# Output projection of a hybrid trunk layer: products in sequence, operands formed earlier, gates eight tiles ahead

## The chip, the cores and the metric

The kernel runs on one core of a Trainium2 chip. The metric is the device time of one execution in microseconds (us). TensorE (PE) does the matrix products, VectorE (DVE) and ScalarE (ACT) the elementwise work, GpSimd (POOL) little besides issuing a few transfers, and SyncE (SP) issues most of them.

## The reference

One layer: two token mixers on a shared normalised input, merged by gates, projected, and followed by a per-layer embedding. All is float32, with 512 tokens and 2048 channels.

```python
h = rmsnorm(x, g_pre)
proj = h @ w_in                        # qkv, z_a, b, a, glu_in, z_b, gate_logits
...                                    # branch A: gated DeltaNet  -> o_a
y_a = o_a @ w_br_a
...                                    # branch B: GLU, depthwise conv, layernorm -> u
y_b = u @ w_br_b
gate_a, gate_b = split(sigmoid(gate_logits + b_gate), 2)
mixed = (gate_a * y_a + gate_b * y_b) @ w_out
x = x + rmsnorm(mixed, g_post)
e = p @ w_ple_proj
x = x + rmsnorm(sigmoid(x @ w_ple_gate) * e, g_ple)
```

The change concerns `gate_b`, `y_b`, the sum of the two gated branches, and the product with `w_out`.

## The kernel before, in words

**Products in float32.** Every operand of a matrix product is split into two halves, hi and lo: ScalarE copies it to the narrower type (hi), VectorE subtracts that from it (lo). A product is then hi·hi + hi·lo + lo·hi, three matmuls of 128 x 512 where one would stand.

**Tiles up to branch B.** `gemm_cm` queues one output tile: 128 channels by 512 tokens, 16 steps of 128 channels with three matmuls each, so 48 matmuls. Its weights come in two loads of 512 KB into the ring `raw`, which has three buffers, and are split into the ring `w`. The queue `jobs` is run in order. While it runs, side work is done by generators: `spawn(gen, period)` adds one, and each matmul of `gemm_cm` counts one tick, so that the generator takes one step every `period` matmuls. Instructions are written engine by engine in the order in which the program emits them; each engine and each queue works through its own in that order, and semaphores hold one that needs what is not there yet. The pools hold a new tile back until the last user of the memory below it is through.

**Branch B.** Two kinds of tiles alternate. `gate_b_tile(i)` multiplies the gate's weights with `hT`, and its evacuation (line 698) forms the sigmoid in a tile `gt` of the pool `slots`. The tile of `w_br_b` multiplies with `uT`, and its evacuation takes the gate times the bank (line 818) and adds it to `mixed[i]`, where the gated branch A lies (line 820). The gates run two tiles ahead of the tiles that use them. `mixed[i]` holds channels 128 i to 128 i + 127 of the sum, 512 tokens wide.

**w_out.** The matrix product with `w_out` is cut into 2 x 2 blocks, of the tokens (halves LO and HI of the columns of `mixed`) and of the channels (0 to 7 and 8 to 15), and seven products do the work of eight. Their names and token operands are P1 (A11), Q5 (S1), P6 (S2), P7 (S3), P3 (S4), P2 (A12) and Q4 (A22), where the S are sums and differences of blocks of `mixed`; their weights are B11 (P1), t = B11 + B12 (Q5), t + B22 (P6), B12 + B22 (P7), B22 (P3), B21 (P2) and t + B22 + B21 (Q4). The output columns are done in two halves, `jp` 0 and 1, and each product of a half has four pieces of weights of 128 x 1024; a piece gives 12 matmuls, so a product gives 48.

A piece passes through these steps. `stage` puts an entry for each of its four quarters q on a list; the entry (`e_a`, `e_b`, `e_c` and so on) issues the loads and sums when the list needs more sources. `load` (line 950) takes a buffer of `raw` for the first two kinds of pieces of half 0 and one of four buffers `rw` behind that; the `rw` and `t` tiles lie in the pool `s3`, which is opened over the space of the pool `s2` of branch B. The sum t is VectorE's (line 964), the blocks B22 and B21 are added to it by accumulating loads on GpSimd's queue (line 956), and P7's sum is VectorE's (line 973). `split_piece` splits a source on ScalarE (line 1010) and VectorE (line 1011) into two tiles `wsp`; three pieces, later four, are split ahead of the matmuls (lines 1034 to 1036, in `mms`).

`run(products, side)` takes the products piece by piece in turn. In half 0 the order before is P1 and Q5 in turn, then P6, P7 and P3 in turn, then P2 and Q4 in turn. The token operands A11 and S1 are formed by `split_a` (line 849 and on, through `sw_split`) when both of their rows of `mixed` are added, S3, S2 and S4 by `split_b` during P1 and Q5, and A12 and A22 by `split_c` during P6, P7 and P3. Behind w_out stand the post-norm, the transposes of its result and the product with `w_ple_gate`.

Of the kernel before, what the change touches and what calls it, by code (L numbers as in the profile page):

```python
# [81 lines left out]
def _body(ctx, tc, A, out):  # L82
# [756 lines left out]
    def split_a():  # L839
        for k2 in range(4):  # L840
            ah = hpool.tile([P, T], F32R, tag="h", name="ah")
            al = hpool.tile([P, T], F32R, tag="h", name="al")
            s1 = slots.tile([P, T], F32, tag="s", name="sf")
            for n in range(2):
                kk = 2 * k2 + n
                while not (kk in added and kk + 8 in added):
                    yield
                c = slice(n * 256, n * 256 + 256)
                nc.vector.tensor_tensor(s1[:, c], mixed[kk][:, HI], mixed[kk + 8][:, HI], ALU.subtract)
                nc.scalar.copy(ah[:, c], mixed[kk][:, LO])  # L850
                nc.vector.tensor_tensor(al[:, c], mixed[kk][:, LO], ah[:, c].bitcast(F32), ALU.subtract)
                yield
            Sf[k2] = s1
            AW["A11"][k2] = (ah, al)
            AW["S1"][k2] = sw_split(hpool, "h", s1)
            yield

    def split_b():
        for k2 in range(4):
            s1 = Sf.pop(k2)  # L860
            s3_ = s3.tile([P, T], F32, tag="s3", name="sf")
            for n in range(2):
                kk = 2 * k2 + n
                c = slice(n * 256, n * 256 + 256)
                nc.vector.tensor_tensor(s3_[:, c], mixed[kk][:, LO], mixed[kk][:, HI], ALU.subtract)
                nc.vector.tensor_tensor(s1[:, c], s1[:, c], mixed[kk][:, LO], ALU.subtract)
            AW["S3"][k2] = sw_split(hpool, "h", s3_)
            yield
            AW["S2"][k2] = sw_split(hpool, "h", s1)
            for n in range(2):  # L870
                kk = 2 * k2 + n
                c = slice(n * 256, n * 256 + 256)
                nc.vector.tensor_tensor(s1[:, c], mixed[kk + 8][:, LO], s1[:, c], ALU.add)
            AW["S4"][k2] = sw_split(slots, "s", s1)
            yield
# [8 lines left out]
    def gate_b_tile(i):  # L884
        gemm_cm(w_in_tile(GATE_TILE0 + 16 + i), hT, evac_gate(gate_b, i, 16 + i))

    gate_b_tile(order[0])
    gate_b_tile(order[1])
# [68 lines left out]

    def e_a(jp, q):
        early[0] = jp == 0
        b11 = load(jp, B11, q)  # L960
# [1 line left out]
        early[0] = False
        t = tb[q] = s3.tile([P, 1024], F32, tag="t", name="t", bufs=4)
        nc.vector.tensor_tensor(t, b11, b12, ALU.add)
        return [b11, t]
# [5 lines left out]
    def sum_t3(jp, q, b22):  # L971
        b12 = load(jp, B12, q)
        nc.vector.tensor_tensor(b12, b12, b22, ALU.add)
        return b12

    def e_b(jp, q):
        acc(tb[q], jp, B22, q)
        b22 = load(jp, B22, q)
        return [tb[q], sum_t3(jp, q, b22), b22]

    def e_p7(jp, q):
        return [sum_t3(jp, q, load(jp, B22, q))]
# [158 lines left out]
    gen = split_c()  # L1141
    ps = run(("P6", "P7", "P3"), stepper(gen))
    drain(gen)
    u2 = [add(unit(S3_, "u2"), ps["P6"][t], s1[t]) for t in range(2)]
# [192 lines left out]
```

## Time and profile before

| | before |
|---|---|
| median of 3 runs | 2548.74 us (2543.42 to 2550.84) |
| profiled execution, its own time | 2548.13 us |
| its span | 2546.4 us |
| granted clock of TensorE, mean | 0.998 |
| TensorE busy | 2503.4 us, 98% of the span |
| VectorE busy | 1650.9 us, 65% |
| ScalarE busy | 1058.2 us, 42% |
| 1840 to 2188, branch B: matmuls, GB/s | 1512, 94 |
| 2188 to 2393, w_out and the post-norm: matmuls, GB/s | 875, 225 |

The span is the stretch from the first to the last instruction that the profile holds; the execution's own time is 1.7 us longer. Times of day in this text are microseconds from the span's start. The matmuls overlap, so their durations (some 0.4 us each) add up to more than the time that passes: what one costs is the spacing of their starts. The granted clock is a share of the full 2.4 GHz; 0.50 is the lower level, 1.2 GHz. Below, w_out begins at 2188.98, right after the last evacuation of branch B.

### The profile page before, as it was taken

What the parts mean: (1) busy time and instruction counts of PE and PEld (TensorE: products, weight loads), DVE (VectorE), ACT (ScalarE), POOL (GpSimd) and SP (SyncE); (2) the same over time, 40 slices, a digit from 0 to 9 for tenths busy, and PEclk for the clock granted to TensorE, in tenths of its full rate; (3) what the DMA queues carried; (4) which work ended last, traced back from release to release, by engine and by line L of the source; (5) the groups of instructions that cost most, each with busy time, mean ns of one, the idle gap of its engine ahead of it and who ended that gap; (6) DMA issues with size and microseconds to landing.
All of it is one profiled execution on the core that took longest, in us unless ns stands there. A gap on an engine that the chain in (4) does not pass through costs nothing.

```text
span 2546.4 us, 32634 instructions
## 1 busy us (share of the span) xinstructions
PE 2503.4 (98%) x12202; PEld 2032.5 (80%) x12202; DVE 1650.9 (65%) x3092; ACT 1058.2 (42%) x2083; POOL 140.4 (6%) x151
## 2 busy tenths in 40 slices
PE   8999999999999999999999999999999999899998
PEld 7878787777878777888888888887888888687886
DVE  6766767666676765977786868947423333787744
ACT  6655455455545545322222222225422222454532
POOL 0100000000000000000000000002000000000000
PEclk9999999999999999999999999999999999999999
DMA  6322222222222222333333333342322223577642
GB/s 256 118 90 71 84 74 80 79 78 84 71 83 72 83 69 81 103 101 106 98 104 100 103 108 96 108 161 91 100 98 93 99 91 99 165 218 213 216 173 75
DMA packets 85406, 279.45 MB, mean 110 GB/s; under 512 B 9472, under 2 KB 9728, under 8 KB 85248
## 3 DMA queue, kind: packets, MB, share of 16 engines
q1 hardware_dynamic: 81792, 266.89, 31.3%
q0 software_dynamic: 2304, 8.39, 1.9%
q10 hardware_dynamic: 1152, 2.10, 0.3%
q8 instruction: 95, 1.56, 0.3%
q14 instruction: 63, 0.52, 0.1%
HBM read 262.66 MB, written 14.68 MB: 109 GB/s over the span
## 4 chain that ended last, share of the span: by engine, by line
PE 84%; DVE 9%; ACT 2%; issue 2%; DMA 2%; POOL 0%; SPq 0%; DVEq 0%; POOLq 0%; ACTq 0%
PE g L180 22%; PE g L178 22%; PE g L176 22%; DVE prod L589 2%; DVE w L124 2%; PE f L1191 2%; PE f L1192 2%; PE f L1190 2%; DVE VT L590 2%; PE psS L467 1%; PE f L1035 1%; PE f L1036 1%; PE f L1034 1%; DVE cv L404 1%; PE psB L462 1%
## 5 line engine op out<-in xcount | busy, mean ns | idle before, releaser
L180 PE MATMUL g<-hh,w 128*128 128x512 f32 x2320 | 919.4, 396 | 13.2 <-DVE w L124 13.2
L178 PE MATMUL g<-hl,w 128*128 128x512 f32 x2320 | 915.9, 395 | 0.0
L176 PE MATMUL g<-hh,w 128*128 128x512 f32 x2320 | 914.5, 394 | 0.0
L124 DVE TENSOR_TENSOR w<-raw,w 128x512 fp32r<-128x512 f32 x780 | 547.8, 705 | 491.8 <-ACT w L123 490.7
L123 ACT CAST w<-raw 128x512 fp32r<-128x512 f32 x780 | 479.1, 620 | 899.2 <-PE g L180 822.6
L180 PEld LDWEIGHTS g<-hh,w 128*128 128x128 f32 x2320 | 436.7, 188 | 107.0 <-DVE w L124 21.4
L178 PEld LDWEIGHTS g<-hl,w 128*128 128x128 f32 x2320 | 436.6, 188 | 87.3 <-issue 1.6
L176 PEld LDWEIGHTS g<-hh,w 128*128 128x128 f32 x2320 | 436.6, 188 | 83.7 <-issue 0.2
L671 DVE SCALAR_TENSOR_TENSOR uc<-sg,vec,uc 128x483 f32<-128x483 f32 (+15 forms) x480 | 351.3, 734 | 14.2 <-ACT uc L668 4.3
L404 DVE SCALAR_TENSOR_TENSOR cv<-g,vec,cv 128x511 f32<-128x511 f32 x144 | 107.0, 743 | 32.9 <-ACT cv L402 32.3
L180 PE MATMUL g<-uh,w 128*128 128x512 f32 x256 | 100.9, 394 | 0.0
L176 PE MATMUL g<-oh,w 128*128 128x512 f32 x256 | 100.9, 394 | 0.0
L178 PE MATMUL g<-ol,w 128*128 128x512 f32 x256 | 100.9, 394 | 0.0
L180 PE MATMUL g<-oh,w 128*128 128x512 f32 x256 | 100.9, 394 | 0.0
L176 PE MATMUL g<-uh,w 128*128 128x512 f32 x256 | 100.9, 394 | 0.0
L178 PE MATMUL g<-ul,w 128*128 128x512 f32 x256 | 100.9, 394 | 0.0
L589 DVE TENSOR_TENSOR prod<-UT,VT 128x2 f32<-128x2 f32 (+30 forms) x248 | 87.8, 354 | 7.2
L1034 PE MATMUL f<-wsp,oph 128*128 128x512 f32 x192 | 74.9, 394 | 3.2 <-ACT wsp L1010 3.2
L1035 PE MATMUL f<-wsp,oph 128*128 128x512 f32 x192 | 75.7, 394 | 1.5 <-DVE wsp L1011 1.5
L1191 PE MATMUL f<-w,xh 128*128 128x512 f32 x192 | 75.1, 391 | 0.1
L1036 PE MATMUL f<-wsp,opl 128*128 128x512 f32 x192 | 75.1, 391 | 0.0
L1192 PE MATMUL f<-w,xl 128*128 128x512 f32 x192 | 75.0, 390 | 0.0
(297 smaller groups left out, 2678.2 us busy)
## 6 DMA issues: line engine op xcount, KB each, us to landing
raw<-in_w_in SPq DMA_DIRECT2D x290, 512.0 KB, 3.3
raw<-in_w_ple_gate SPq DMA_DIRECT2D x40, 512.0 KB, 4.0
rw<-in_w_out SPq DMA_DIRECT2D x36, 512.0 KB, 5.0
raw<-in_w_br_a SPq DMA_DIRECT2D x32, 512.0 KB, 3.3
raw<-in_w_br_b SPq DMA_DIRECT2D x32, 512.0 KB, 3.2
t<-in_w_out POOLq DMA_DIRECT2D x16, 512.0 KB, 7.3
x<-in_x SPq DMA_DIRECT2D x8, 512.0 KB, 9.4
pe_dram<-e_sb SPq DMA_DIRECT2D x16, 256.0 KB, 5.6
```

Source lines behind the costliest of these rows:

```text
L123: nc.scalar.copy(hi, rq)
L124: nc.vector.tensor_tensor(lo, rq, hi.bitcast(F32), ALU.subtract)
L176: mm(ps, wh, rh, start=(k == 0), stop=False)
L178: mm(ps, wh, rl, start=False, stop=False)
L180: mm(ps, wl, rh, start=False, stop=(k == NK - 1))
L404: nc.vector.scalar_tensor_tensor(y[:, s:], ps[:, 0:T - s], vv(w0 + 3 - s), y[:, s:], ALU.mult, ALU.add)
L589: nc.vector.tensor_tensor(pv_, um, vm, ALU.mult)
L671: nc.vector.scalar_tensor_tensor(y[:, s:], u[:, 0:T - s], vv(w0 + TAPS - 1 - s), y[:, s:], ALU.mult, ALU.add)
L1035: mm(ps, lh, wl[:, c], start=False, stop=False)
L1036: mm(ps, ll, wh[:, c], start=False, stop=kk == 7)
L1191: mm(ps[tt], lh, wl, start=False, stop=False)
L1192: mm(ps[tt], ll, wh, start=False, stop=k == NK - 1)
```

## The change

- The gates run eight tiles ahead (`AHEAD = 8`) and, but for the first two, lie in the pool `s2`.
- `split_a`, `split_b` and `split_c` become `combine(k2)`, which forms all token operands of two rows of `mixed` and their partners but the split of S3. The generator over `combine(0)` to `combine(2)` starts behind the ninth of the 16 tiles of `w_br_b` (all gates are through by then), with a step every 12 matmuls; `combine(3)` runs during P1, three steps a piece; the splits of S3 run during P2.
- The order of half 0 is now P1, P2, Q5, P6, P7, P3, Q4, one product after the other. P1's piece is B11 and P2's is B21, both without a sum.
- The sum t is no longer formed from two loaded pieces on the way to Q5, but during P2: B12 is loaded into the t tile itself (line 979), and the kept piece of P1 is added to it (line 980). P7 loads B22 and B12 for itself (line 1000 is its sum), P3 loads B22 again.
- The first nine pieces' splits, before eight, lie in the ring `w` and in `wx`; the second load of x goes to `slots`, before to `hpool`.

The diff, cut to its core:

```diff
-    def evac_gate(dst, i, col):
+    def evac_gate(dst, i, col, pool=None):
         def f(ps):
-            gt = slots.tile([P, T], F32, tag="s", name="gt")
+            gt = (pool or slots).tile([P, T], F32, tag="s2" if pool else "s", name="gt")
...
+    def combine(k2):
+        ah = hpool.tile([P, T], F32R, tag="h", name="ah")
+        al = hpool.tile([P, T], F32R, tag="h", name="al")
+        for kk, c in halves(k2):
+            while not (kk in added and kk + 8 in added):
+                yield
+            nc.scalar.copy(ah[:, c], mixed[kk][:, LO])
+            nc.vector.tensor_tensor(al[:, c], mixed[kk][:, LO], ah[:, c].bitcast(F32), ALU.subtract)
+            yield
+        AW["A11"][k2] = (ah, al)
+        for kk, c in halves(k2):
+            CC[kk] = sw_split(hpool, "h", mixed[kk + 8])
+            yield
+        s1 = slots.tile([P, T], F32, tag="s", name="sf")
+        for kk, c in halves(k2):
+            nc.vector.tensor_tensor(s1[:, c], mixed[kk][:, HI], mixed[kk + 8][:, HI], ALU.subtract)
+        AW["S1"][k2] = sw_split(hpool, "h", s1)
+        yield
+        s3_ = slots.tile([P, T], F32, tag="s", name="sf")
+        s4 = slots.tile([P, T], F32, tag="s", name="sf")
+        for kk, c in halves(k2):
+            nc.vector.tensor_tensor(s3_[:, c], mixed[kk][:, LO], mixed[kk][:, HI], ALU.subtract)
+            nc.vector.tensor_tensor(s1[:, c], s1[:, c], mixed[kk][:, LO], ALU.subtract)
+        yield
+        for kk, c in halves(k2):
+            nc.vector.tensor_tensor(s4[:, c], mixed[kk + 8][:, LO], s1[:, c], ALU.add)
+        AW["S2"][k2] = sw_split(slots, "s", s1)
+        yield
+        AW["S4"][k2] = sw_split(slots, "s", s4)
+        Sf[k2] = s3_
+        yield
...
     jobs.append(finish)
+    for n in range(2, AHEAD):
+        gate_b_tile(order[n], s2)
     for n, i in enumerate(order):
-        if n + 2 < NK:
-            gate_b_tile(order[n + 2])
-        elif n == NK - 2:
-            jobs.append(lambda: spawn(split_a(), 6, "mix"))
         gemm_cm(A["w_br_b"][i], uT, evac_yb(i))
+        if n + AHEAD < NK:
+            gate_b_tile(order[n + AHEAD], s2)
+        elif n + AHEAD == NK:
+            jobs.append(lambda: spawn(split_mixed(), 12, "mix"))
...
+    def e_p1(jp, q):
+        early[0] = True
+        first[q] = load(jp, B11, q)
+        early[0] = False
+        return [first[q]]
+
+    def e_p2_t1(jp, q):
+        b21 = load(jp, B21, q)
+        t = t_tile(q)
+        nc.sync.dma_start(t, WO[jp, B12, q])
+        nc.vector.tensor_tensor(t, t, first.pop(q), ALU.add)
+        return [b21]
...
-            if n < 8:
+            if n < 9:
...
-                xr[tt, j] = unit(HP_, "xr")
+                xr[tt, j] = unit(SLOT, "xr")
...
-    for e, jp in ((e_a, 0), (e_b, 0), (e_c, 0), (e_a, 1), (e_63, 1), (e_p2, 1), (e_p7, 1), (e_t, 1)):
+    for e, jp in ((e_p1, 0), (e_p2_t1, 0), (e_t, 0), (e_p6, 0), (e_p7, 0), (e_p3, 0), (e_q4, 0), (e_a, 1), (e_63, 1), (e_p2, 1), (e_p7, 1), (e_t, 1)):
         stage(e, jp)
...
-    gen = split_b()
-    ps = run(("P1", "Q5"), stepper(gen))
+    gen = combine(3)
+    ps = run(("P1",), stepper(gen, 3))
     drain(gen)
     s1 = [snap(S3_, x) for x in ps["P1"]]
-    s5 = [snap(S3_, x) for x in ps["Q5"]]
+    gen = split_s3()
+    ps = run(("P2",), stepper(gen))
+    drain(gen)
+    c11 = [add(unit(S3_, "c11"), ps["P2"][t], s1[t]) for t in range(2)]
...
+    ps = run(("Q5",))
+    s5 = [snap(S3_, x) for x in ps["Q5"]]
+    ps = run(("P6",))
...
```

**Place 1.** SP's loads at the end of branch B and the start of w_out. `raw` are pieces of the ring with three buffers, `rw` and `t` pieces in `s3`; the numbers count tiles. Before:

```order
L950 DMA raw_17421<-in_w_out 128x1024
L950 DMA raw_17423<-in_w_out 128x1024
L950 DMA raw_17431<-in_w_out 128x1024
L950 DMA rw_17585<-in_w_out 128x1024
L950 DMA rw_17587<-in_w_out 128x1024
L950 DMA raw_17433<-in_w_out 128x1024
L950 DMA raw_17468<-in_w_out 128x1024
L950 DMA rw_17680<-in_w_out 128x1024
```

and in the changed kernel:

```order
L956 DMA raw_17480<-in_w_out 128x1024
L956 DMA raw_17482<-in_w_out 128x1024
L956 DMA raw_17488<-in_w_out 128x1024
L956 DMA rw_17524<-in_w_out 128x1024
L979 DMA t_17526<-in_w_out 128x1024
L956 DMA rw_17562<-in_w_out 128x1024
L979 DMA t_17564<-in_w_out 128x1024
L956 DMA rw_17593<-in_w_out 128x1024
L956 DMA raw_17494<-in_w_out 128x1024
L979 DMA t_17595<-in_w_out 128x1024
L956 DMA rw_17618<-in_w_out 128x1024
```

Three raw loads stand ahead in both. Before, raw loads of the next pieces follow behind two loads of P7 and P3; now the fourth raw load, P1's last piece, stands behind three rw loads of P2 and two loads of B12 into t tiles.

**Place 2.** VectorE from the last evacuation of branch B on. Line 818 is the gate times the bank, line 820 the last addition to `mixed`, 1011 (before) and 1034 (after) the low half of a piece of weights. Before:

```order
L1011 TENSOR_TENSOR wsp_17428<-raw_17421,wsp_17427 128x1024
L818 TENSOR_TENSOR gt_17159<-g_17330,gt_17159 128x512
L964 TENSOR_TENSOR t_17425<-raw_17421,raw_17423 128x1024
L820 TENSOR_TENSOR gt_13133<-gt_13133,gt_17159 128x512
L1011 TENSOR_TENSOR wsp_17442<-raw_17431,wsp_17441 128x1024
L849 TENSOR_TENSOR sf_17357<-gt_10733,gt_13133 128x256
L1011 TENSOR_TENSOR wsp_17438<-t_17425,wsp_17437 128x1024
```

and in the changed kernel, where nine rows are left out (the split of P1's third piece and eight instructions of `combine(3)`):

```order
L818 TENSOR_TENSOR gt_16824<-g_17406,gt_16824 128x512
L1034 TENSOR_TENSOR wsp_17491<-raw_17482,wsp_17490 128x1024
L820 TENSOR_TENSOR gt_13133<-gt_13133,gt_16824 128x512
...
L980 TENSOR_TENSOR t_17526<-t_17526,raw_17480 128x1024
L836 TENSOR_TENSOR opl_17591<-sf_17557,oph_17589 128x512
L1034 TENSOR_TENSOR wsp_17599<-rw_17562,wsp_17598 128x1024
L980 TENSOR_TENSOR t_17564<-t_17564,raw_17482 128x1024
L1034 TENSOR_TENSOR wsp_17530<-raw_17494,wsp_17529 128x1024
L1034 TENSOR_TENSOR wsp_17568<-rw_17524,wsp_17567 128x1024
```

The sum t stood right behind the last evacuation; now the first sum stands behind the operand work, and the split of P1's fourth piece (`raw_17494`) behind the second sum. The sum reads `raw_17480`, whose buffer that fourth piece takes.

**Place 3.** VectorE ahead of Q5's last piece in the changed kernel, `t_17620`. Line 1083 adds P1 to P2, line 1103 multiplies with g_post, line 1000 is a sum of P7's weights:

```order
L1083 TENSOR_TENSOR c11_17705<-f_17627,snap_17614 128x512
L1034 TENSOR_TENSOR wsp_17720<-t_17595,wsp_17719 128x1024
L1083 TENSOR_TENSOR c11_17707<-f_17628,snap_17616 128x512
L1000 TENSOR_TENSOR rw_17843<-rw_17843,rw_17841 128x1024
L1103 TENSOR_TENSOR c11_17705<-c11_17705,grow_17709 128x512
L1103 TENSOR_TENSOR c11_17707<-c11_17707,grow_17709 128x512
L1034 TENSOR_TENSOR wsp_17725<-t_17620,wsp_17724 128x1024
```

and before, around one of P7's sums (there line 973):

```order
L1011 TENSOR_TENSOR wsp_17712<-rw_17682,wsp_17711 128x1024
L836 TENSOR_TENSOR opl_17665<-sf_17357,oph_17663 128x512
L973 TENSOR_TENSOR rw_17736<-rw_17736,rw_17734 128x1024
L836 TENSOR_TENSOR opl_17709<-gt_11033,oph_17707 128x512
L1011 TENSOR_TENSOR wsp_17740<-rw_17680,wsp_17739 128x1024
```

A sum of P7 now stands ahead of a split that Q5, two products earlier, needs.

## Rows read from the trace of the kernel before

**Rows 1.** Page, busy us of each engine, share of the span, instructions.

```profile
PE 2503.4 (98%) x12202; PEld 2032.5 (80%) x12202; DVE 1650.9 (65%) x3092; ACT 1058.2 (42%) x2083; POOL 140.4 (6%) x151
```

**Rows 2.** Windows: stretch, its us, busy us of engines, granted clock, DMA share, GB/s.

```profile
2100.00:2150.00 50.00, 50.00 (x219) 40.78 (x218) 16.58 (x27) 13.02 (x23) 0.00 (x0) 1.00 0.29 95
2150.00:2200.00 50.00, 47.98 (x204) 37.66 (x203) 30.53 (x55) 17.70 (x29) 1.06 (x1) 1.00 0.41 131
2200.00:2250.00 50.00, 45.55 (x193) 35.74 (x193) 45.42 (x60) 29.32 (x39) 6.07 (x7) 1.00 0.82 214
2250.00:2300.00 50.00, 50.00 (x220) 41.05 (x220) 36.85 (x41) 26.03 (x39) 5.20 (x6) 1.00 0.76 220
```

**Rows 3.** All waits of TensorE, 1840 to 2320: us in total, times, longest.

```profile
PE f L1034 <- ACT wsp L1010: 3.9, 4, 2.0
PE f L1035 <- DVE wsp L1011: 1.5, 2, 1.0
PE f L1034 <- DVE gt L818: 0.9, 1, 0.9
```

**Rows 4.** TensorE's timeline: start, us, instruction, [idle before <-releaser].

```profile
2188.98 0.47 PE L1034 MATMUL f<-wsp,ah 128*128 128x512 f32 x1 [0.88 <-DVE gt L818]
...
2204.63 0.74 PE L1034 MATMUL f<-wsp,oph 128*128 128x512 f32 x2 [2.03 <-ACT wsp L1010]
...
2340.55 0.44 PE L1113 MATMUL x1t<-cst,snap 128*128 128x128 f32 x2 [2.38 <-DVE snap L1107]
```

**Rows 5.** ScalarE's group, 2188 to 2320: count | busy, mean ns | idle before.

```profile
L1010 ACT CAST wsp<-t 128x1024 fp32r<-128x1024 f32 x20 | 21.0, 1050 | 26.9 <-PE f L1035 10.8 <-DVE t L964 8.8 <-PE f L1036 7.2
```

**Rows 6.** VectorE's timeline at the seam of branch B and w_out.

```profile
2188.75 1.22 DVE L964 TENSOR_TENSOR t<-raw 128x1024 f32<-128x1024 f32 x1
2189.88 0.68 DVE L820 TENSOR_TENSOR gt<-gt 128x512 f32<-128x512 f32 x1
2190.48 1.22 DVE L1011 TENSOR_TENSOR wsp<-raw,wsp 128x1024 fp32r<-128x1024 f32 x1
2191.61 0.42 DVE L849 TENSOR_TENSOR sf<-gt 128x256 f32<-128x256 f32 x1
```

**Rows 7.** SP's timeline at the seam.

```profile
2167.11 11.58 SPq L950 DMA_DIRECT2D raw<-in_w_out  x3
2188.18 0.81 SPq L950 DMA_DIRECT2D rw<-in_w_out  x2
2190.03 0.80 SPq L950 DMA_DIRECT2D raw<-in_w_out  x2
```

**Rows 8.** DMA issues at 2188.1, 2190.0 and 2190.8: KB each, us to landing.

```profile
rw<-in_w_out SPq DMA_DIRECT2D x1, 512.0 KB, 3.5
...
raw<-in_w_out SPq DMA_DIRECT2D x1, 512.0 KB, 5.5
...
rw<-in_w_out SPq DMA_DIRECT2D x1, 512.0 KB, 7.3
```

**Rows 9.** A window behind a longer wait, in an earlier stage.

```profile
954.00:957.00 3.00, 3.00 (x9) 2.32 (x8) 2.08 (x5) 2.90 (x5) 0.00 (x0) 0.50 0.51 175
```

**Rows 10.** TensorE's timeline there, first and last of ten matmuls.

```profile
953.47 0.61 PE L180 MATMUL g<-hh,w 128*128 128x512 f32 x1 [2.83 <-DVE w L124]
...
957.22 0.40 PE L180 MATMUL g<-hh,w 128*128 128x512 f32 x1
```

**Rows 11.** DMA issues 2219.5 to 2221 and 2207 to 2207.5.

```profile
grow<-in_g_post ACTq DMA_DIRECT2D x2, 256.0 KB, 7.5
rw<-in_w_out SPq DMA_DIRECT2D x1, 512.0 KB, 6.9
...
t<-in_w_out POOLq DMA_DIRECT2D x1, 512.0 KB, 5.4
```

**Rows 12.** DMA issues 2280 to 2292.

```profile
t<-in_w_out POOLq DMA_DIRECT2D x4, 512.0 KB, 8.8
rw<-in_w_out SPq DMA_DIRECT2D x3, 512.0 KB, 16.2
```

More of the change, by code (lines that the diff above doesn't have):

```diff
@@ L837, in sw_split @@
         return hi, lo
-    def split_a():
-        for k2 in range(4):
[L841 to L875, printed above, removed]
@@ L877, in split_c, with halves @@
-    def split_c():
-        for kk in range(8):
-            CC[kk] = sw_split(*((slots, "s") if kk < 4 else (s3, "s3")), mixed[kk + 8])
+    def halves(k2):
+        for n in range(2):
+            yield 2 * k2 + n, slice(n * 256, n * 256 + 256)
+    def combine(k2):
[29 more added lines that the diff above has]
+        yield
@@ L880, in split_c, with split_mixed, split_s3, gate_b_tile @@
+    def split_mixed():
+        for k2 in range(3):
+            yield from combine(k2)
+    def split_s3():
+        for k2 in range(4):
+            AW["S3"][k2] = sw_split(s3, "s3", Sf.pop(k2))
             yield
     order = [k + 8 * n for k in range(8) for n in range(2)]
[L884 to L888, printed above, removed]
+    AHEAD = 8
+    def gate_b_tile(i, pool):
+        gemm_cm(w_in_tile(GATE_TILE0 + 16 + i), hT, evac_gate(gate_b, i, 16 + i, pool))
@@ L956, in acc, with t_tile, e_p6 @@
         nc.gpsimd.dma_start(t, WO[jp, blk, q], accum_op=ALU.add)
+    first = {}
+    def t_tile(q):
+        tb[q] = s3.tile([P, 1024], F32, tag="t", name="t", bufs=4)
+        return tb[q]
+    def e_p1(jp, q):
[9 more added lines that the diff above has]
+        return [b21]
     def e_a(jp, q):
-        early[0] = jp == 0
         b11 = load(jp, B11, q)
         b12 = load(jp, B12, q)
[L962 to L965, printed above, removed]
+        nc.vector.tensor_tensor(t_tile(q), b11, b12, ALU.add)
+        return [b11, tb[q]]
+    def e_p6(jp, q):
+        acc(tb[q], jp, B22, q)
+        return [tb[q]]
     def e_63(jp, q):
@@ L969, in e_63, with e_p7, e_p3 @@
         return [tb[q], load(jp, B22, q)]
-    def sum_t3(jp, q, b22):
+    def e_p7(jp, q):
+        b22 = load(jp, B22, q)
         b12 = load(jp, B12, q)
         nc.vector.tensor_tensor(b12, b12, b22, ALU.add)
[L974 to L982, printed above, removed]
+        return [b12]
+    def e_p3(jp, q):
+        return [load(jp, B22, q)]
     def e_p2(jp, q):
@@ L986, in e_p2, with e_q4 @@
         return [load(jp, B21, q)]
+    def e_q4(jp, q):
+        acc(tb[q], jp, B21, q)
+        return [tb[q]]
     def e_t(jp, q):
         return [tb[q]]
-    def e_c(jp, q):
-        return e_p2(jp, q) + [tb[q]]
     def split_piece():
@@ L1129, in drain @@
             pass
-    for e, jp in ((e_a, 0), (e_b, 0), (e_c, 0), (e_a, 1), (e_63, 1), (e_p2, 1), (e_p7, 1), (e_t, 1)):
+    for e, jp in ((e_p1, 0), (e_p2_t1, 0), (e_t, 0), (e_p6, 0), (e_p7, 0), (e_p3, 0), (e_q4, 0), (e_a, 1), (e_63, 1), (e_p2, 1), (e_p7, 1), (e_t, 1)):
         stage(e, jp)
-    gen = split_b()
-    ps = run(("P1", "Q5"), stepper(gen))
+    gen = combine(3)
+    ps = run(("P1",), stepper(gen, 3))
     drain(gen)
     s1 = [snap(S3_, x) for x in ps["P1"]]
-    s5 = [snap(S3_, x) for x in ps["Q5"]]
+    gen = split_s3()
+    ps = run(("P2",), stepper(gen))
+    drain(gen)
+    c11 = [add(unit(S3_, "c11"), ps["P2"][t], s1[t]) for t in range(2)]
     gp = [bcast_row(A["g_post"], j) for j in (0, 1)]
     fin = out_fin(0, gp)
[L1141 to L1144, printed above, removed]
+    for t in range(2):
+        fin(t, 0, c11[t])
+    ps = run(("Q5",))
+    s5 = [snap(S3_, x) for x in ps["Q5"]]
+    ps = run(("P6",))
+    u2 = [add(s1[t], ps["P6"][t], s1[t]) for t in range(2)]
     d = [minus(unit(S3_, "d"), s5[t], u2[t]) for t in range(2)]
+    ps = run(("P7",))
     u3 = [add(u2[t], ps["P7"][t], u2[t]) for t in range(2)]
     for t in range(2):
+        fin(2 + t, 1, minus(s5[t], s5[t], u3[t]))
+    ps = run(("P3",))
+    for t in range(2):
         fin(t, 1, add(d[t], ps["P3"][t], d[t]))
-        fin(2 + t, 1, minus(s5[t], s5[t], u3[t]))
-    ps = run(("P2", "Q4"))
-    for t in range(2):
-        fin(t, 0, add(s1[t], ps["P2"][t], s1[t]))
+    ps = run(("Q4",))
     for t in range(2):
```

2 lines of the change are left out of this document (added).

## The prediction

> **What bounds the kernel now.** I read the busy shares first: TensorE is busy 98% of the span [rows 1], so only its waits can be won. The table by windows then shows where they lie around the change: no loss through branch B, the loss in 2150 to 2250, none in 2250 to 2300 [rows 2]. The waits of TensorE name who ended them [rows 3], and its timeline gives the places [rows 4]: 0.9 us at the start of w_out, then short waits for split pieces of weights in the first two products (P1, Q5, piece by piece in turn), the longest 2.03, six of them after the first. Together these are 6.3 us [rows 3]. By counts it is more: the two windows hold 204 and 193 matmuls where undisturbed ones hold 219 and 220, 42 too few, at 50/220 = 0.227 us 9.5 us [rows 2]. A few records can be missing, and a matmul after a wait is followed by longer spacing, so I take 9.0: 1.0 at the start and 8.0 behind. That is the most this change can win there, 0.3% of the time. A later 2.4 us, before the transposes of x1 [rows 4], waits on the post-norm chain, which stays.
>
> **The change part by part.**
>
> *Gates eight tiles ahead.* The same 32 tiles of 48 matmuls run in another order. All waits of TensorE from 1840 to 2320 are the three lines of [rows 3], none of them in branch B, and VectorE and ScalarE are busy 16.6 and 13.0 of 50 us there [rows 2]. Cost 0.
>
> *Operands formed in branch B.* Three of four combinations move ahead of w_out. One is, on VectorE, five instructions of 512 columns at 0.68 and ten of 256 at 0.42 [rows 6], 7.6 us, and less on ScalarE. Three are 23 us of VectorE in the seven tiles that follow (seven times 48 matmuls at 0.227, 76 us), where two thirds of it is free: cost 0; if that cover were gone a piece would be late by one such instruction, 0.7. What it takes out of 2187 to 2225 is what made pieces late there: VectorE was busy 45.4 of 50 [rows 2]. So those six waits go: minus 8.0.
>
> *What is late next: the fourth piece of P1.* P1 alone now needs 36 matmuls for its first three pieces, 36 x 0.227 = 8.2 us from 2188.98 [rows 4], so the fourth is due at 2197.2. Its load goes into a raw buffer, of which there are three; the first three hold the pieces 0 to 2, and buffer 0 is now read once more, by the sum t = B12 + B11 (line 980), which waits for a new load of B12. Before, B12's load had come in the same raw ring long before, and the sum stood right behind the last evacuation [rows 6]. Now (order of SP and VectorE, places 1 and 2):
> - The loads into rw and t now lie over space that held a gate: they wait for the last addition of branch B, line 820. In VectorE's order a 1024-wide split stands ahead of it, as the sum did before, so it ends at 2189.88 + 0.68 = 2190.6 [rows 6]. Before, the first rw load went at 2188.18 [rows 7].
> - First load at 2190.6, t's at 2191.0 (issues stand 0.4 apart [rows 7]). A load issued alone took 3.5, and the third and the fifth in line landed at 2190.0 + 5.5 and 2190.9 + 7.3, 1.35 for each place [rows 8]. So t lands at 2195.5.
> - VectorE ahead of the sum: the split of piece 2 after ScalarE's 1.05 (to 2192.8), then operand work of 0.6, 0.6, 4 x 0.34 and 0.6 (starts in a row stand that much closer than the durations [rows 6]), to 2196.0; the sum takes 1.22 and ends at 2197.2 [rows 6].
> - The raw load goes at 2197.2, sixth in the queue: 2190.6 + 3.5 + 5 x 1.35 = 2200.8, and alone it would need 3.5, 2200.7.
> - ScalarE splits a piece of t ahead of it, which waits for the second sum (t, fourth in the queue, lands at 2198.2; a split on VectorE and the sum end at 2200.4): 2201.4, then its own 1.05: 2202.5 [rows 5]. VectorE's low half comes 1.22 later, 2203.7 [rows 6].
> - TensorE waits from 2197.2 to 2202.5, 5.3, runs two matmuls, and waits again to 2203.7, 0.7: together 6.0. Bounds: 4 if the splits ahead cost nothing (2200.8 to the first matmul, and half of the rest), 8 if the loads share the engines with other traffic and land 2 us later.
>
> Here a page can be set beside the row. Loads queued on SP landed 1.35 us apart [rows 8]. The Trainium skill's DMA: Bandwidth & Descriptors, Anatomy of one DMA, fits a transfer by 2.0 us and its bytes over 436 GB/s, measured on the GpSimd path; taken as an estimate for SP's loads that is 1.2 us each and 2.0 once. By it the sixth load would land at 2199.8, but not before the sum lets it go, 2197.2 + 3.2 = 2200.4: the wait would be about 0.4 us shorter. No run here shows 436 GB/s on such a load.
>
> *The clock.* The short waits left the granted clock at 1.00 [rows 2]. The one wait of 2.83 us, at 953, did not: the clock stood at 0.50, which is the lower level, for 954 to 957 [rows 9], and the matmuls from 953.47 to 957.22, nine spacings, took 3.75 us instead of 2.04, so 1.7 us [rows 10]. A wait of 5.5 us should do the same. I take 1.7, with 0 and 2 as bounds (part of it can fall inside the wait).
>
> *The queue of sums behind.* Four more loads of 512 KB (B12 comes twice), 4 x 1.35 us of queue. P7's sums (line 1000) each wait for two loads, and the third stands ahead of Q5's last split on VectorE (place 3). One of its loads needs a buffer that the second sum frees, and that sum one that the split of P2's last piece frees: eight VectorE instructions of 1.13 and one of 0.6 (their spacing in [rows 6]) behind 2202.5 in the order, 2212.2; its load 3.5 to 4 later, its sum at 2217.2, 28.2 us into w_out. With an accumulating load and two g_post rows in flight a load took 6.9 [rows 11], so it lands at 35.1; its sum 1.2, g_post's two products 1.2 and the split 1.2 make 38.7. TensorE, after 132 matmuls, needs it at 6.0 + 1.7 + 132 x 0.227 = 37.7. So 1.0; bounds 0 (landing in under 6) and 4. P7's third piece is held the same way by the fourth sum, with some 2 us to spare after it; 0.5, bounds 0 and 4.
>
> *Kept or nothing.* The start still waits for the last evacuation: the first bank is its bank, 1.0 as before. Matmuls and splits are as many as before. x's second load goes to other buffers and into other places of SP's order; the product before the transposes may wait, bounds minus 1 and plus 2, taken 0.
>
> **Sum**, against the profiled execution's 2548.13 (the span 2546.4 plus 1.7 around it): minus 8.0, plus 6.0, 1.7, 1.0 and 0.5, is plus 1.2: 2549.3. The median of the runs shown, 2548.74, lies 0.6 above that execution, so 2549.9; I say 2550.
>
> **Rivals.** A measurement of this kernel tells about 0.3%, 7.6 us, from no change: faster is below 2541.1, slower above 2556.4.
>
> *It does what it says.* The pieces of both products are there in time and w_out runs from its start: 2548.7 - 8.0 = 2540.7. For it: three raws land well before the start as now (three loads over 2167 to 2178 [rows 7]), and the operands are ready. It needs the fourth raw load to go at 2188 and not behind the sum. Against it: the order, where SP has that load behind rw and t loads that cannot go before branch B ends, and the re-read of buffer 0.
>
> *Loads collide.* The sums of P7 stand in VectorE's order ahead of splits of earlier products. If their loads meet the accumulating loads, several of which are now issued within a few us, TensorE waits for a load. Three loads issued over 2280 to 2292 had a median of 16.2 us to landing beside four accumulating ones at 8.8 [rows 12]. With 16.2 in place of 6.9 the wait at Q5's last piece is 1.0 + 9.3: 2559. It decides from some 13 us to landing on. Against it: before, such loads at up to 16 us fell into 2250 to 2300, at 220 GB/s, and TensorE lost nothing there [rows 2]. The Trainium skill, Trainium Kernel Development and Optimization, Key Constraints, has DMAs of all queues run on the same 16 engines and interleave, which is this rival's ground; the 5.4 us of an accumulating load alone against 8.8 among others agrees [rows 11, 12].
>
> **How the numbers follow.** Forecast 0.77, from 2545 to 2556 by its bounds, all of it within 0.3%. It does what it says 0.07: faster 0.05, the rest within. Loads collide 0.16: slower. So faster 0.05, same 0.79, slower 0.16. The range takes in most of both rivals' near sides: 2544.5 to 2558.
>
> **What would show it.** The waits of TensorE in the first 35 us of w_out: right, if the six short ones are gone and one of 4.5 to 7 us stands at P1's fourth piece, ended by ScalarE's split, with that load issued some 9 us into w_out right after the first sum; and if the granted clock falls to 0.50 behind it. Q5's last split should end a wait of 0 to 4. Wrong, if the fourth raw load goes with the first rw loads, if P1 has no wait over 2 us, or if a wait over 3 us stands in branch B or beyond P7.

## The result, and the profile after

The changed kernel takes 2554.28 us (median of 11 runs, 2549.91 to 2558.34), the kernel before 2547.28 in the same runs. The ratio is 1.0027, with a 95% interval of 1.0018 to 1.0036: 5 to 9 us slower. The forecast was 2550, the range 2544.5 to 2558. The profiled execution took 2554.67, its span is 2552.9 us and its mean granted clock 0.996.

The waits of TensorE in half 0 (the columns are those of [rows 3]) show the six short ones gone and two long ones in their place, the first where the forecast had it:

```profile
PE f L1057 <- ACT wsp L1033: 5.3, 1, 5.3
PE f L1058 <- DVE wsp L1034: 4.1, 2, 3.6
PE f L1057 <- DVE gt L818: 0.9, 1, 0.9
```

Its timeline has the places, as [rows 4] had them before: the start of w_out, P1's last piece, Q5's last piece, and at the end of w_out two waits close together.

```profile
2186.50 0.47 PE L1057 MATMUL f<-wsp,ah 128*128 128x512 f32 x1 [0.88 <-DVE gt L818]
2200.34 1.22 PE L1057 MATMUL f<-wsp,ah 128*128 128x512 f32 x2 [5.32 <-ACT wsp L1033]
2228.22 0.80 PE L1058 MATMUL f<-wsp,oph 128*128 128x512 f32 x1 [3.59 <-DVE wsp L1034]
...
2342.22 0.50 PE L1058 MATMUL f<-wsp,oph 128*128 128x512 f32 x1 [1.35 <-DVE wsp L1034]
...
2344.80 0.69 PE L1136 MATMUL x1t<-cst,c 128*128 128x128 f32 x2 [1.38 <-DVE c L1130]
```

Windows behind these waits have the clock at its lower level, called the half clock below (the third number from the end, 0.50). Before, it stayed at 1.00 all through w_out, up to 2300 by [rows 2] and from 2300 to 2400 by two more such windows.

```profile
2201.00:2203.50 2.50, 2.46 (x7) 1.51 (x6) 2.50 (x3) 0.23 (x1) 0.00 (x0) 0.50 0.87 354
2228.50:2231.00 2.50, 2.50 (x7) 1.92 (x8) 2.50 (x3) 0.24 (x1) 1.96 (x3) 0.50 0.46 56
2346.00:2350.00 4.00, 4.00 (x14) 3.28 (x13) 3.56 (x6) 1.39 (x3) 0.00 (x0) 0.50 0.53 183
```

What each product loses is counted from the starts in TensorE's timeline: 48 matmuls at an undisturbed spacing of 0.2286 us take 10.97 us, and what 48 starts take beyond that is the loss, waits and half clock together. Loss in us, in the order of each kernel; "end" are the last two of w_out's 14 products, among which the transposes stand, so that their own time is in it. The start's 1.0 is in none.

| kernel | half 0 by product | half 0 | end |
|---|---|---|---|
| before | P1 and Q5 in turn 7.3, then 0.7 | 8.0 | 6.1 |
| changed | P1 7.5, P2 0, Q5 5.2, P6 0, P7 1.1, P3 0, Q4 0 | 13.7 | 9.5 |
| changed, second profile (e8) | P1 8.5, Q5 5.6, P7 0.3 | 14.3 | 8.2 |
| e1 | P1 0.1, P2 1.3, P7 4.7 | 6.1 | 5.7 |
| e2 | P1 7.8, P7 0.3 | 8.1 | 5.2 |
| e3 | P1 and Q5 in turn 9.0 | 9.0 | 4.7 |
| e4 | P1 7.5, Q5 4.7, P7 1.7 | 13.8 | 7.3 |
| e5 | P1 0.1, P2 1.0, P7 3.8 | 4.8 | 6.0 |
| e6 | P1 0.1, P7 5.3 | 5.3 | 5.5 |
| e7 | P1 8.2, Q5 2.0, P7 4.8 | 15.0 | 7.3 |
| e9 | P1 0.1, P7 and P3 in turn 1.9 | 2.0 | 9.3 |
| e10 | P1 8.6, P7 and P3 in turn 1.2 | 9.8 | 6.5 |
| e11 | P1 and Q5 in turn 9.2, then 1.4 | 10.5 | 4.9 |
| e12 | P1 0.1, P7 and P3 in turn 1.9 | 2.0 | 5.1 |

So of the two profiled executions the changed one loses 5.7 us more in half 0 and 3.4 more at the end, 9.1; from the start of w_out to the end of the span it is 366.4 against 357.4. The spans differ by 6.5 only, since w_out began at 2186.50 instead of 2188.98. That is no gain of the change: branch B takes the same time in both, the 2.4 us stand before it, where the same work runs, and over all the profiles here w_out began between 2186.5 and 2189.5. Some 1.6 of the 2.4 are the half clock behind the wait of 2.83 us at 953 [rows 9, 10]. The changed kernel's execution has the same wait there, and behind it the clock stayed at 1.00:

```profile
952.65 0.50 PE L180 MATMUL g<-hh,w 128*128 128x512 f32 x1 [2.76 <-DVE w L124]
...
952.50:956.00 3.50, 3.35 (x15) 2.77 (x16) 2.55 (x6) 2.72 (x4) 0.00 (x0) 1.00 0.41 150
```

In the 14 profiles this wait is 2.74 to 2.85 us long; the half clock stands behind it in eleven and not in three (changed, e4, e10). So a half clock behind a wait of this size can differ between executions of the same work, and part of a difference between two rows of the table is that.

### The profile page after: what moved, and what is told of

The parts are those of the page before. It is cut to its first block, busy times and chain, and to the rows that moved or that the text cites. A ratio compares the mean times of both kernels' runs of the same rounds, so it can differ in the third digit from the quotient of the medians.

```text
span 2552.9 us, 32648 instructions
## 1 busy us (share of the span) xinstructions
PE 2506.6 (98%) x12202; PEld 2036.1 (80%) x12202; DVE 1652.8 (65%) x3092; ACT 1062.4 (42%) x2083; POOL 140.6 (6%) x151
## 4 chain that ended last, share of the span: by engine, by line
PE 84%; DVE 9%; issue 3%; ACT 2%; DMA 2%; POOL 0%; SPq 0%; DVEq 0%; POOLq 0%; ACTq 0%
PE g L180 22%; PE g L178 22%; PE g L176 22%; DVE prod L589 2%; DVE w L124 2%; PE f L1221 2%; PE f L1220 2%; PE f L1219 2%; DVE VT L590 2%; PE psS L467 1%; PE f L1058 1%; PE f L1057 1%; DMA rw<-in_w_out 1%; PE f L1059 1%; DVE cv L404 1%
## 5 line engine op out<-in xcount | busy, mean ns | idle before, releaser
L671 DVE SCALAR_TENSOR_TENSOR uc<-sg,vec,uc 128x483 f32<-128x483 f32 (+15 forms) x480 | 351.7, 735 | 14.3 <-ACT uc L668 4.3
```

Of the source, the lines that this page charges most:

```text
L671: nc.vector.scalar_tensor_tensor(y[:, s:], u[:, 0:T - s], vv(w0 + TAPS - 1 - s), y[:, s:], ALU.mult, ALU.add)
```

## The experiments

The ratios are to the kernel before, timed on the same chip.

**e1, P1's fourth piece.**

```diff
     def e_p1(jp, q):
-        early[0] = True
+        early[0] = q < 3
```

> The changed kernel, with P1's fourth piece loaded into an rw buffer in place of a raw one, so that its load need not wait for the first sum t = B12 + B11. In the order that this gives, the three first sums of P7 also fall behind Q5's last split. Theory (each of the two new stalls stands by itself): P1's wait of 5.3 us with the half clock behind it, 7.5 us together, goes, and so does the 5.2 us at Q5's last piece; about 2554.3 - 12.7 = 2541.6, 0.9978 of before. Rival (given back): the rw buffer that P1's piece now holds until the fourth sum delays P7's loads, and the time comes back as a wait at P6 or P7; 2550 or more.

2545.08 us, ratio 0.9993 (0.9984 to 1.0001), by the two ratios some 9 less than the changed kernel. P1's loss falls from 7.5 to 0.1 and Q5's from 5.2 to 0, the latter by VectorE's order, which the edit moved too; 4.7 come back at P7, 1.6 of them half clock. There a sum waits for a load that took 8.7 us, and the splits of P7's first pieces stand behind it (VectorE's timeline):

```profile
2232.85 1.22 DVE L1000 TENSOR_TENSOR rw<-rw 128x1024 f32<-128x1024 f32 x1 [4.85 <-DMA rw<-in_w_out]
2234.00 2.35 DVE L1034 TENSOR_TENSOR wsp<-rw,wsp 128x1024 fp32r<-128x1024 f32 x2
```

Theory for the two stalls, rival for a third of what they cost.

**e2, the order of one sum.**

```diff
+    lows = []
...
-        nc.vector.tensor_tensor(b12, b12, b22, ALU.add)
+        with tc.issue_after(lows[11]) if (jp, q) == (0, 2) else ExitStack():
+            nc.vector.tensor_tensor(b12, b12, b22, ALU.add)
...
-        nc.vector.tensor_tensor(lo, src, hi.bitcast(F32), ALU.subtract)
+        lows.append(nc.vector.tensor_tensor(lo, src, hi.bitcast(F32), ALU.subtract).ins)
```

> The changed kernel, with P7's third sum queued behind the low half of Q5's last piece on VectorE, nothing else. Theory: Q5's last split was late only because it stood behind a sum that waited 7.1 us for a load, so the 3.6 us wait and the half clock behind it, 5.2 us, go: 2554.3 - 5.2 = 2549.1, and P1's 5.3 us stay. Rival: the split's own piece, or P7's third piece behind it, is late as well, and the wait moves to P6 or P7: 2553 or more.

2547.94, ratio 1.0006 (0.9997 to 1.0015): by the two ratios some 5 less than the changed kernel. Q5's loss is gone, P1's stays, nothing moves behind. One sum put behind one split on VectorE was worth these 5.2 us; the load itself took 9.8 here, and TensorE did not wait for it.

**e3, operands early, products as before.** The gates, `combine` and `split_s3` of the changed kernel; entries and `run` calls of the one before:

```diff
-    gen = split_b()
-    ps = run(("P1", "Q5"), stepper(gen))
+    def rest():
+        yield from combine(3)
+        yield from split_s3()
+    gen = rest()
+    ps = run(("P1", "Q5"), stepper(gen, 3))
...
```

> The kernel before in its w_out (P1 and Q5 in turn, sums t from two loaded pieces, P6, P7, P3 in turn), with the gates eight ahead and three quarters of the operands formed in branch B as in the changed kernel. Theory of the prediction (VectorE's operand work made the six short waits): they go, 8 us: 2547.3 - 8 = 2539.3, 0.9969 of before. Rival (the three raw buffers and the landing of their loads made them): most of them stay, 2547.3 - 2 = 2545.3 or nothing.

2548.51, ratio 1.0001 (0.9992 to 1.0010). Most of the short waits stay, five of 4.6 us in all instead of six of 5.4 [rows 3]:

```profile
PE f L1040 <- ACT wsp L1016: 4.1, 4, 2.3
PE f L1040 <- DVE gt L818: 0.9, 1, 0.9
PE f L1041 <- DVE wsp L1017: 0.5, 1, 0.5
```

The rival holds: SP's raw loads went at 2189.3, 2195.5 and 2203.1, each when a raw buffer came free, and VectorE's sums t waited for them, in the first 25 us of w_out as long as before (VectorE's groups, before and e3; the last column is the idle time in front):

```profile
L964 DVE TENSOR_TENSOR t<-raw 128x1024 f32<-128x1024 f32 x4 | 4.9, 1223 | 3.9 <-DMA raw<-in_w_out 3.9
...
L970 DVE TENSOR_TENSOR t<-raw 128x1024 f32<-128x1024 f32 x4 | 4.9, 1224 | 3.7 <-DMA raw<-in_w_out 3.7
```

Two limits: e3 takes away what the change takes away, and no more. In these 25 us VectorE's work on operands falls from 9.6 to 7.4 us only (in the first 36 from 15.1 to 7.4). And the 9.0 in the table hold some 3 us of half clock, behind the wait of 2.3, which the kernel before does not have. Without it the profile loses 6, against 8.0 before: the operands' work can have cost some 2 of the 8, the late raw pieces the rest. The medians show no gain.

**e4, the home of x's second load.**

```diff
-                xr[tt, j] = unit(SLOT, "xr")
+                xr[tt, j] = unit(HP_, "xr")
```

> The changed kernel, with x's second load in hpool as before instead of slots. Theory A (the 3.4 us lost at the last product and its transposes come from x's loads, which now go at the same time as P7's last weights): the loss goes, 2554.3 - 3.4 = 2550.9. Theory B (they come with the order of loads and sums of P7's last pieces, whatever x does): no change, 2554.3. P1's and Q5's waits stay in both.

2554.36, ratio 1.0026 (1.0015 to 1.0036): the time is that of theory B. The profile is less clear: x's first eight loads went at 2281 to 2291 here and at 2296 to 2310 in the changed kernel, and with them VectorE's order moved, the split of P7's last piece ahead of Q4's first as in the kernel before. TensorE does not wait for that split, and waits 2.25 us at the transposes (2.38 before). The loss at the end is 7.3, between the changed kernel's 9.5 and before's 6.1, and unlike before a half clock stands in it.

**e5, P7's sums in program order.** As e1, and:

```diff
-        nc.vector.tensor_tensor(b12, b12, b22, ALU.add)
+        tc.keep_in_program_order(nc.vector.tensor_tensor(b12, b12, b22, ALU.add))
```

> P1's fourth piece in an rw buffer as in the run e1, and besides each of P7's sums kept on VectorE behind what the program writes before it (the splits of the pieces ahead of it), in both halves. Theory (what e1 gave back, 4.7 us in P7, is again a split that stands behind a sum that waits for a load): it goes, 2545.1 - 4.7 = 2540.4, 0.9974 of before. Rival (P7's pieces are late by their loads, whatever the order): the 4.7 stay or come back at P7's third piece; 2545 or more.

2546.09, ratio 0.9996 (0.9987 to 1.0005): nothing won over e1. The rival: P7 still loses 3.8, and its sum now waits 6.86 us for its load. Behind w_out stands a wait of 1.8 us that e1 does not have; the rule held in half 1 too.

**e6, P2's loads first.** As e5, with the loads of t 0 and 1 issued with P2's third piece, those of 2 and 3 with its fourth:

```diff
-        t = t_tile(q)
-        nc.sync.dma_start(t, WO[jp, B12, q])
-        nc.vector.tensor_tensor(t, t, first.pop(q), ALU.add)
+        for r in {2: (0, 1), 3: (2, 3)}.get(q, ()):
+            t = t_tile(r)
+            nc.sync.dma_start(t, WO[jp, B12, r])
+            nc.vector.tensor_tensor(t, t, first.pop(r), ALU.add)
```

> As e5, and P2's loads of B21 ahead of B12's loads into the t tiles, which follow with P2's third and fourth piece. Theory (P2's 1.3 us of waits in e1 come from loads that stand behind those of t in SP's queue): they go, 2540.4 - 1.3 = 2539.1. Rival (the sums t now come too late for Q5): Q5's first pieces wait, and the time is that of e5 or more.

2545.95, ratio 0.9997 (0.9988 to 1.0006). P2's loss is 0 as expected. P7's is 5.3 in place of 3.8, though its waits are as long as in e5 (3.0 and 2.9 us): the rest is a half clock that e5 does not have.

```profile
2243.50:2246.50 3.00, 3.00 (x9) 2.32 (x8) 3.00 (x5) 1.99 (x2) 0.00 (x0) 0.50 0.89 292
```

So P7's pieces are late by their loads here too (its sum waits 6.8 us for one), whatever was won ahead of them.

**e7, fewer accumulating loads.**

```diff
     def e_p6(jp, q):
-        acc(tb[q], jp, B22, q)
+        if q in (0, 3):
+            acc(tb[q], jp, B22, q)
```

> The changed kernel without the accumulating loads of P6's second and third piece of half 0 (B22 is left out of these two), which are in flight beside the load that P7's third sum waits for. The sum still stands ahead of Q5's last split. Theory (the load took 9.3 us, not the 6.9 of the prediction, for a second accumulating load beside it): it takes under 7, the wait at Q5's last piece is under 1.3 us, no half clock behind it: 2554.3 - 4 = 2550. Rival (the g_post rows beside it make it, or it was late for its issue): the load stays over 8.5 and the wait over 2.5 us; 2554.

2553.88, ratio 1.0026 (1.0015 to 1.0037). The load took 7.7, with one accumulating load beside it, in place of 9.3 (9.2 in e8 and 8.4 in e4, which have it as in the changed kernel), and Q5's loss fell from 5.2 to 2.0, without the half clock; so the second accumulating load was part of it, though not all the way to the 7 expected. The time did not fall: P7's next load was issued while three accumulating ones were under way and took 10.3 us, and P7 lost 4.8, half clock included. This is the DMA view of 2229 to 2237 (KB each, median us to landing; the first of the four had landed at 2235.8, the last line's load went at 2236.8):

```profile
t<-in_w_out POOLq DMA_DIRECT2D x4, 512.0 KB, 8.8
rw<-in_w_out SPq DMA_DIRECT2D x1, 512.0 KB, 10.3
```

**e8, the changed kernel again**, without an edit.

> The changed kernel once more, for a second profile. Theory (the 3.4 us lost at the last product and its transposes belong to the change): the last two products of w_out lose 9 us again. Rival (they belong to the one execution that was profiled): they lose 5 to 7, as before, where it is 6.1. The waits at P1's and Q5's last pieces are there in both.

2555.63 in its one run. The end loses 8.2 (9.5 in the first profile), P1 8.5 and Q5 5.6: the stalls belong to the change, and the loss at the end came again, less 1.3.

**e9, P7 and P3 in turn.** As e6 without e5's rule, and:

```diff
-    def e_p3(jp, q):
-        return [load(jp, B22, q)]
+    def e_73(jp, q):
+        b22 = load(jp, B22, q)
+        b12 = load(jp, B12, q)
+        nc.vector.tensor_tensor(b12, b12, b22, ALU.add)
+        return [b12, b22]
...
-    ps = run(("P7",))
+    ps = run(("P7", "P3"))
...
-    ps = run(("P3",))
```

> As e6 (P1's fourth piece in an rw buffer, P2's loads ahead of t's) without its rule on P7's sums, and P7 and P3 piece by piece in turn, so that P7's sum and P3 share one load of B22 as in the kernel before: four loads of 512 KB fewer, and a piece of P7 wanted every 24 matmuls instead of 12. Theory (what e1, e5 and e6 gave back at P7, 4 to 5 us, is the rate of its loads, two for a piece of 2.7 us): no wait in half 0 but the 1.0 at the start, so 8 us less than before: 2546.8 - 8 = 2538.8, 0.9969 of before. Rival (the accumulating loads crowd what stands beside them): a wait of 2 to 5 us at Q5, P7 or P3 again; 2543 or more.

2540.18, ratio 0.9972 (0.9962 to 0.9982): faster than both; 7 us less than before. Half 0 loses 2.0, in one wait:

```profile
PE f L1062 <- DVE wsp L1038: 1.6, 1, 1.6
PE f L1061 <- DVE gt L818: 0.9, 1, 0.9
```

With four loads fewer and a piece of P7 wanted half as often, what e1, e5 and e6 gave back is kept; which of the two does it was not taken apart. By the two ratios e9 is 14 us less than the changed kernel, about the sum of what e1 and e10 bring alone.

**e10, the same alone.** The changed kernel with the edit of e9's diff only.

> The changed kernel with P7 and P3 in turn and one load of B22 for both, nothing else (in this order no sum of P7 stands directly ahead of Q5's last split any more but the first two). P1's 7.5 us stay. Theory: Q5's 5.2 us and P7's 1.0 go, 2554.3 - 6.2 = 2548.1. Rival: they move behind; 2552 or more.

2550.02, ratio 1.0004 (0.9994 to 1.0014), 4 to 6 less than the changed kernel: between the theory's 2548.1 and the rival's 2552. In the profile Q5's loss is gone, 1.2 is left at P7 and P3, and P1's 8.6 stay.

**e11, the gates alone.** The kernel before with the hunks on `evac_gate`, `AHEAD` and `gate_b_tile`.

> The kernel before with the gates eight tiles ahead, in the pool s2, and nothing else. Theory (32 tiles of 48 matmuls in another order cost nothing): 2546.8, within 0.1%. Rival (the loads of w_out that must wait for the last gate come later, so its first pieces are late): 2 us or more slower, with longer waits at P1 and Q5.

2548.61, ratio 1.0005 (0.9996 to 1.0013): too close to tell 0 from 2 us. Its profile is in the rival's direction: SP's first rw load went 0.7 us behind the start of w_out in place of 0.8 ahead of it, and one wait at a piece of Q5 is 3.7 in place of 2.0. Half 0 loses 2.5 more, 1.6 of it half clock.

**e12, the last splits by hand.** As e9, and in half 1:

```diff
+    lows = []
...
-        nc.vector.tensor_tensor(lo, src, hi.bitcast(F32), ALU.subtract)
+        with tc.issue_after(lows[-1]) if n == 52 else ExitStack():
+            lows.append(nc.vector.tensor_tensor(lo, src, hi.bitcast(F32), ALU.subtract).ins)
...
-                nc.vector.scalar_tensor_tensor(x1[tt][j], x1[tt][j], rm[:, n:n + 1], xr.pop((tt, j)), ALU.mult, ALU.add)
+                with tc.issue_after(lows[51]) if tts == LOW else ExitStack():
+                    nc.vector.scalar_tensor_tensor(x1[tt][j], x1[tt][j], rm[:, n:n + 1], xr.pop((tt, j)), ALU.mult, ALU.add)
```

> As e9, and in half 1 VectorE's order at the end of w_out is set by hand: the split of P7's last piece ahead of that of Q4's first (the changed kernel and e9 have them the other way round, the kernel before has them this way), and the products of x1 with the norm's factor behind it. Theory (part of what the end of w_out loses, 9.5 us in the changed kernel and 9.3 in e9 against 6.1 before, is this order: a wait of 1.6 us for P7's last split, one of 1.5 at the transposes, and the half clock behind them): both waits fall under 1 us and no half clock, e9's 2540.2 - 3 = 2537, 0.996 of before. Rival (the late landing of P7's last load alone makes it): the loss stays 8 us or more and the time that of e9, 2540.

2540.00, ratio 0.9970 (0.9959 to 0.9980). In the profile part of the theory holds: the end loses 5.1 against e9's 9.3, without the wait for P7's last split and without the half clock; the wait at the transposes stays at 1.5. P7's last load was also less late here, 0.26 us of waiting at its sum against 0.81 in e9, so the order is not alone in it. The medians show nothing: the time is the rival's, that of e9. e9's profiled execution, 2543.92, was 3.7 above its median, so the loss at the end was probably large in that execution and smaller in most.

## Why the prediction was right, and where not

*The six short waits go: minus 8.0.* Measured: the 8.0 of before is gone from where it stood. But the reason given, VectorE's work on operands, is wrong for most of it: e3 moved that work as the change does and kept most of the waits, so the number came out right by luck. Before, the longest of the six, 2.03 us, stood behind a sum t that waited 1.8 us for a raw load; the busy share of 45.4 in 50 us [rows 2] was read as the cause, where ScalarE's waits for t [rows 5] and the rows on SP's raw loads [rows 7, 8] were nearer to it. That the waits are gone because P1 and P2 need no sum and three raw pieces lie ready is argued from the order; no run has the new order of products alone.

*P1's fourth piece: 6.0 and the clock 1.7.* Measured 7.5, and 8.5 in the second profile, and it went by the steps. Only the second short wait of 0.7 is not there: the two matmuls ahead of it ran at the half clock and took up the time. The first sum ended at 2195.05, and the raw load went at once (SP's timeline, VectorE's timeline, and the DMA view of the first, fifth and raw load):

```profile
2188.17 0.33 SPq L956 DMA_DIRECT2D rw<-in_w_out  x1
...
2195.13 0.33 SPq L956 DMA_DIRECT2D raw<-in_w_out  x1
```

```profile
2193.83 1.22 DVE L980 TENSOR_TENSOR t<-t,raw 128x1024 f32<-128x1024 f32 x1
...
2197.04 1.22 DVE L980 TENSOR_TENSOR t<-t,raw 128x1024 f32<-128x1024 f32 x1
```

```profile
rw<-in_w_out SPq DMA_DIRECT2D x1, 512.0 KB, 3.7
...
rw<-in_w_out SPq DMA_DIRECT2D x1, 512.0 KB, 7.0
...
raw<-in_w_out SPq DMA_DIRECT2D x1, 512.0 KB, 3.8
```

The load went 8.6 us into w_out (8.2 forecast). First and fifth load landed at 2191.9 and 2197.0, 1.27 apart for each place, where the prediction took 1.35 from [rows 8]. The Trainium skill's fit that it set beside the row (DMA: Bandwidth & Descriptors, Anatomy of one DMA) gives an estimate of 1.2 us for each load. The 0.4 us that the prediction takes off the wait by it follows the raw load's landing, 2200.8, which in its own steps does not decide: ScalarE's split ahead ends at 2201.4. e1 takes away the one thing that held the load, and the wait is gone. The clock's 1.7 was taken from the one half clock behind a wait of 2.83 us [rows 9, 10]; that wait alone did not promise it, as the changed kernel's own row at 952 shows, but behind the 5.3 us here it came in every profile that has this wait.

*Q5's last piece: 1.0, bounds 0 to 4.* This is the step that failed: 5.2 measured, 5.6 in the second profile. The order and the chain were as described, and the second of P7's sums ended at 2215.2, 28.7 us into w_out, where the prediction had it at 28.2. The load that then went, at 2215.2, took longer, and the half clock behind the wait was not counted:

```profile
2213.97 1.23 DVE L1000 TENSOR_TENSOR rw<-rw 128x1024 f32<-128x1024 f32 x1 [0.57 <-DMA rw<-in_w_out]
...
2224.60 1.23 DVE L1000 TENSOR_TENSOR rw<-rw 128x1024 f32<-128x1024 f32 x1 [7.07 <-DMA rw<-in_w_out]
2225.74 1.29 DVE L1103 TENSOR_TENSOR c<-c,grow 128x512 f32<-128x512 f32 x2
2226.94 4.63 DVE L1034 TENSOR_TENSOR wsp<-t,wsp 128x1024 fp32r<-128x1024 f32 x4
```

```profile
t<-in_w_out POOLq DMA_DIRECT2D x2, 512.0 KB, 8.6
grow<-in_g_post ACTq DMA_DIRECT2D x2, 256.0 KB, 9.3
rw<-in_w_out SPq DMA_DIRECT2D x1, 512.0 KB, 9.3
```

9.3 us, where [rows 11] had 6.9: 2.4 more, which with the half clock's 1.4 makes most of the 4.2 that were missing. The prediction put the 6.9 beside one accumulating load; GpSimd's timeline before has two there as well, but earlier:

```profile
2216.38 0.88 POOL L956 DMA_DIRECT2D t<-in_w_out  x1 [8.31 <-DVE opl L836]
2217.87 0.87 POOL L956 DMA_DIRECT2D t<-in_w_out  x1 [0.61 <-DVE wsp L1011]
```

They landed 1.3 and 4.9 us behind that load's issue at 2220.7. In the changed kernel one landed 6.7 us behind the load's issue, and the other, issued 2.0 us after it, was beside it to its end. So it is not the count of accumulating loads alone; e7 shows that one fewer shortens it. The rival "loads collide" named this place and this mechanism, and set the point from which it decides at 13 us to landing; 9.3 were enough for 5.2 us.

*P7: 0.5.* 1.1 in one profile, 0.3 in the other. Within its bounds. The four more loads are there, but their reason in the prediction is not: B12 came twice before too, for t and for P7's sum; what is loaded once more is B22, for P3, and that is what e9 and e10 take away again.

*The end of w_out: 0, bounds minus 1 and plus 2.* 3.4 and 2.1 more than before in the two profiles, so outside the bounds. The prediction looked at the transposes' wait and at x's loads; where x lies as before (e4) the time does not fall. What the trace shows is P7's last sum waiting for its load, and behind it the split of a piece of Q4, `t`, ahead of P7's last, `rw`:

```profile
2337.99 1.23 DVE L1000 TENSOR_TENSOR rw<-rw 128x1024 f32<-128x1024 f32 x1 [2.25 <-DMA rw<-in_w_out]
...
2339.81 1.21 DVE L1034 TENSOR_TENSOR wsp<-t,wsp 128x1024 fp32r<-128x1024 f32 x1
2340.94 1.22 DVE L1034 TENSOR_TENSOR wsp<-rw,wsp 128x1024 fp32r<-128x1024 f32 x1
```

Before, the last sum waited for its load too, but the two splits stood the other way round, and TensorE did not wait for P7's:

```profile
2333.14 1.23 DVE L973 TENSOR_TENSOR rw<-rw 128x1024 f32<-128x1024 f32 x1 [1.30 <-DMA rw<-in_w_out]
...
2335.49 1.22 DVE L1011 TENSOR_TENSOR wsp<-rw,wsp 128x1024 fp32r<-128x1024 f32 x1
...
2336.70 1.21 DVE L1011 TENSOR_TENSOR wsp<-t,wsp 128x1024 fp32r<-128x1024 f32 x1
```

e2 has the changed order too, but its last sum came without a wait, and its end loses 5.2; so TensorE's wait of 1.35 takes the late load and the order together. That wait alone is cheap, since the one at the transposes is shorter for it. e10 has the late load, the order and both waits, but not the half clock, and its end loses 6.5 (TensorE's timeline, and a window behind it):

```profile
2338.94 0.50 PE L1061 MATMUL f<-wsp,oph 128*128 128x512 f32 x1 [1.30 <-DVE wsp L1037]
...
2341.52 0.44 PE L1139 MATMUL x1t<-cst,c 128*128 128x128 f32 x2 [1.39 <-DVE c L1133]
```

```profile
2339.00:2346.00 7.00, 5.61 (x28) 4.34 (x29) 6.38 (x9) 2.13 (x3) 1.56 (x1) 1.00 0.33 112
```

So of the 3.4 and 2.1 some 3.0 and 1.7, what they lose beyond e10, are the half clock. How late P7's last load lands differs between the profiles, and so does the clock behind it; why is open, and so is how much of the end's loss is in the medians.

*Gates and operands: 0.* No wait in branch B, and its length is unchanged. The gates' 0 for w_out is not shown: e11's time leaves anything from none to 3 us, and its profile has the loads into rw later by 1.5 us.

*The sum.* plus 1.2 forecast; by the two profiles 9.1 in w_out: minus 8.0, plus 7.5, 5.2, 1.1, and 3.4 at the end. By the medians it is 7.0. The forecast, a change of less than 0.3%, held by a little (1.0027), and not as no change: the interval, 1.0018 to 1.0036, tells it from 0. Of its terms P1's was right by its mechanism, the minus 8.0 by luck, and two were too small, Q5's and the end's.

## What to carry to other kernels

A sum or a split that waits for a load holds everything written behind it on its engine: look in the order for instructions of a later product ahead of an earlier one, and count what the half clock takes behind a long stall. A load that is free in the plan still costs its place among the loads. Taking one stall away can move time to the next late load, but need not: e1's two stalls cost 12.7 us and 4.7 of it came back at P7, while of e2's 5.2 nothing did. What worked best here, e9, takes four loads away and spreads their use as well. And two profiles that differ by 1.5 to 3 us may differ by a half clock alone: look for it before a cause is named.
